# A decoder layer on one core: evacuation and background steps issued ahead of the weight split in each chunk

## The chip, the cores and the metric

The kernel runs on one core of a Trainium2 chip. The metric is the device time of one execution in microseconds (us), as the median of several runs. Before the change it is 2984.26 us (three runs, 2979.92 to 2984.27).

A core has a matrix engine (TensorE, PE in the profile, with its weight loads as PEld), a vector engine (VectorE, DVE), a scalar engine (ScalarE, ACT), GpSimd (POOL) and SyncE (SP), from whose queue nearly all DMAs of this kernel are issued. Each engine takes its instructions in the order in which the program wrote them, and waits on semaphores for what others owe it.

## The reference

One layer of a decoder, for 256 prompt tokens and 8 x 8 sample tokens, 320 token columns in all, with a model width of 2048:

```python
def swiglu(x, w_in, w_out):
    gate, up = jnp.split(x @ w_in, 2, axis=-1)
    return (jax.nn.silu(gate) * up) @ w_out

def token_mixer(h, w_in, ...):
    qk_pre, mv, mo, mif, aq, ak, av, gm, ga = split_cols(h @ w_in)
    # branch A: causal conv and SiLU of qk_pre, then a chunkwise mLSTM
    # branch B: dilated causal attention, of the prompt and over the cache
    merged = jax.nn.sigmoid(gm) * (hm @ w_pm) + jax.nn.sigmoid(ga) * (ha @ w_pa)
    return merged @ w_out, ...

x = x + 0.5 * swiglu(rmsnorm(x, ln_ffa), w_ffa_in, w_ffa_out)
x = x + token_mixer(rmsnorm(x, ln_mix), ...)
x = x + 0.5 * swiglu(rmsnorm(x, ln_ffb), w_ffb_in, w_ffb_out)
y = rmsnorm(x, ln_f)
```

Beside y, the new keys and values, the mLSTM state and the last convolution rows are returned.

## The kernel before

**Foreground.** Every product with a weight matrix is cut into jobs (`add_job`): a job gives 256 output columns for all 320 tokens, in one PSUM tile `fg` (two of them take turns). A job runs over its weights in chunks of up to four 128-row tiles, 512 KB of float32. `load_upto` fetches a chunk into one of four `raw` tiles. `split_upto` splits it into two parts that the matrix engine can take at full rate: ACT casts `raw` to `hi` (L223), DVE subtracts to get `lo` (L224); there are three `hi` and three `lo` tiles. For each tile pair PE then runs three matmuls (hi by x-high, hi by x-low, lo by x-high), so a full chunk has 24. The token side is split likewise: `xh`, `xl` for w_in, `hh`, `hl` in the feed-forward blocks, and `bh`, `bl` (`split_act`, L1345 and L1346) for the products with w_pm and w_pa.

**Order inside a chunk.** Nothing reorders the program; `run_job` (L270) writes it by hand. For chunk number ci it writes: the DMAs that were put off (`run_later`), the split of chunk ci+2, the background steps, then, in a job's first chunk (n == 0), the job's `setup` and the evacuation of the job before (`flush_evac`), then the load of chunk ci+6, then the matmuls of chunk ci. The load of ci+6 goes into the `raw` tile that the split of ci+2 read, so SP waits for that `lo`. The `hi` tile of chunk ci+2 is the one that chunk ci-1 read, so ACT waits for PE there.

**Background.** Everything else is written as Python generators that advance by one stage at each step: list `every` in each chunk, `even` and `odd` in alternate chunks, `slow` in 8 of 15. They carry the attention over the cache (`sample_attention`: `kd` transposes at L626, `qbd` at L674, scores `ss` from L701 on), the mLSTM (`mlstm`: state `C` at L1167, `ks`, `qm`, `kw`) and the later stages of evacuations. `flush_evac` runs an evacuation up to its first `yield` and puts the rest into `every`. Two kinds matter here:

- `sigmoid_evac` (20 jobs: mo, gm, ga): DVE multiplies by `rstd` (L395, tile `sg`), ACT takes an exponential (L998), POOL adds one (L999); then after a yield DVE takes the reciprocal of one half (L1002), after another yield that of the other.
- `mv_evac` (four jobs) and its like: DVE multiplies by `rstd` (L395, tile `mv`), two yields, then PE transposes the result (`tok_major`, L332).

**Openings.** The products with w_pm and w_pa begin with a `setup` (`pm_open`, `pa_open`) that splits the mLSTM's result `hr` and the attention's result `ar`. The first of four pieces of each is split earlier by a generator (`presplit`); the other three are split by `take` (L1356) in the setup itself.

**Sequence.** Feed-forward block a (chunks 0 to 271), the mixer's projection w_in with nearly all background work (272 to 448), w_pm (449 to 464), w_pa (465 to 480), w_out, feed-forward block b. In the first five chunks `first_chunk` stands in the place of the split and prepares the input.

Of the kernel before, what the change touches and what calls it, by code (L numbers as in the profile page):

```python
# [128 lines left out]
def decoder_kernel(tc, I, O, K):  # L129
# [13 lines left out]
    def mm(out, a, b, start=True, stop=True, **kw):  # L143
        T.matmul(out, a, b, start=start, stop=stop, **kw)  # L144
# [16 lines left out]
    def run_later(force=False):  # L161
        rest = []
        for e in later_q:
            e[0] -= 1
            if e[0] <= 0 or force:
                e[1]()
            else:
                rest.append(e)
        later_q[:] = rest
# [4 lines left out]
    def step(lst):  # L174
        for g in list(lst):
            try:
                next(g)
            except StopIteration:
                lst.remove(g)

    def spawn(g, lst=None, first=False):
        lst = every if lst is None else lst
        lst.insert(0 if first else len(lst), g)

    RAWB, HLB, KRB = 4, 3, 3
# [4 lines left out]
    def load_upto(n):  # L190
        while st["loaded"] < min(n, len(chunks)):
            i = st["loaded"]
            src, nk, kind = chunks[i]
            t = wp.tile([128, 4, 256], F32, tag="raw", bufs=RAWB, name="raw")
            if kind == "mif":
                v = t.rearrange("p a b -> p (a b)")[:, :128].rearrange("p (k c) -> p k c", k=16)
                dma(v, src)
            else:
                dma(t[:, :nk], src)
            raw[i] = t  # L200
            st["loaded"] += 1

    def split_upto(n):
        while st["split"] < min(n, len(chunks)):
            i = st["split"]
            load_upto(i + 1)
            src, nk, kind = chunks[i]
            hi = wp.tile([128, 4, 256], F32R, tag="hi", bufs=HLB, name="hi")
            lo = wp.tile([128, 4, 256], F32R, tag="lo", bufs=HLB, name="lo")
            t = raw.pop(i)  # L210
            if kind == "mif":
                G.memset(hi.bitcast(F32), 0.0)
                G.memset(lo.bitcast(F32), 0.0)
                r = t.rearrange("p a b -> p (a b)")[:, :128].rearrange("p (k c) -> p k c", k=16)
                h = hi.rearrange("p a b -> p (a b)").rearrange("p (k c) -> p k c", k=16)
                l = lo.rearrange("p a b -> p (a b)").rearrange("p (k c) -> p k c", k=16)
                for o, s in ((0, 0), (32, 4)):
                    S.copy(h[:, :, o:o + 4], r[:, :, s:s + 4])
                    V.tensor_tensor(l[:, :, o:o + 4], r[:, :, s:s + 4], h[:, :, o:o + 4].bitcast(F32),
                                    op=OP.subtract)  # L220
                wh[i], wl[i] = h, l
            else:
                S.copy(hi[:, :nk], t[:, :nk])  # L223
                V.tensor_tensor(lo[:, :nk], t[:, :nk], hi[:, :nk].bitcast(F32), op=OP.subtract)  # L224
                wh[i], wl[i] = hi, lo
            st["split"] += 1
# [22 lines left out]
    def fg_tile():  # L249
        return pp.tile([128, 2, 512], F32, tag="fg", bufs=2, name="fg")  # L250
# [7 lines left out]
    def flush_evac():  # L258
        if pending[0] is not None:
            evac, ps = pending[0]  # L260
            pending[0] = None
            g = evac(ps)
            if g is not None:
                try:
                    next(g)
                    every.append(g)
                except StopIteration:
                    pass

    def run_job(job):  # L270
        cs, nkt, mov, evac, kind, setup = job
        ps = fg_tile()
        for n, (ci, k0, nk) in enumerate(cs):
            run_later()
            if ci < 5:
                first_chunk(ci, 0)
            else:
                split_upto(ci + HLB)
            if tick[0] % 2 == 0:
                step(even)  # L280
            else:
                step(odd)
            tick[0] += 1
            pace[0] += 8
            if pace[0] >= 15:
                pace[0] -= 15
                step(slow)
            step(every)
            if n == 0 and setup is not None:
                setup()  # L290
            if ci == 7 or (n == 0 and ci != 4):
                flush_evac()
            load_upto(ci + HLB + RAWB)
            h, l = wh.pop(ci), wl.pop(ci)
            for m in range(1 if kind == "mif" else 2):
                if m and ci < 3:
                    first_chunk(ci, 1)
                for k in range(nk):
                    xh, xl = mov(k0 + k)
                    if kind == "mif":  # L300
                        a, b, out = h[:, k], l[:, k], ps[0:64, 0, 0:NT]
                    else:
                        a, b, out = h[:, k, m * 128:(m + 1) * 128], l[:, k, m * 128:(m + 1) * 128], ps[:, m, 0:NT]
                    first, last = k0 + k == 0, k0 + k == nkt - 1
                    mm(out, a, xh, start=first, stop=False)
                    mm(out, a, xl, start=False, stop=False)
                    mm(out, b, xh, start=False, stop=last)
        pending[0] = (evac, ps)
# [1024 lines left out]
    for j in range(8):  # L1333
        add_job(w_in, 0, 16, C_GA + j * 256, mov_x, lambda ps, j=j: sigmoid_evac(ps, gate_d[8 + j]),
                setup=(lambda: spawn(presplit("hr"))) if j == 7 else None)
# [15 lines left out]
    def presplit(key):  # L1351
        while key not in M:
            yield
        PRE[key] = split_act(M[key][0], t_tile)
# [5 lines left out]
    def pm_setup(j):  # L1360
        if j == 7:
            spawn(presplit("ar"))
        if j == 0:
            pm_open()
        load_pair(j, gate_d[j], t_tile(F32, "sg"))

    def pa_setup(j):
        if j == 0:
            pa_open()
        load_pair(j, gate_d[8 + j], ft_tile("sg"))  # L1370
# [56 lines left out]
    for j in range(8):  # L1427
        add_job(I["w_pm"][0], 0, 8, j * 256, mov_b, lambda ps, j=j: pm_evac(ps, j),
                setup=lambda j=j: pm_setup(j))
    for j in range(8):  # L1430
        add_job(I["w_pa"][0], 0, 8, j * 256, mov_b, lambda ps, j=j: pa_evac(ps, j),
                setup=lambda j=j: pa_setup(j))
# [57 lines left out]
    def warm(n):  # L1490
        ps = bg_tile()
        for _ in range(n):
            mm(ps[:, 0:128], ones, ones)
# [7 lines left out]
    def prep_pair(j, fg=False):  # L1501
        xv, c0, g0 = xl[j // 2], (j % 2) * 256, G_FFA + 2 * j
        X[j] = fp.tile([128, 2, NT], F32, tag="x", bufs=8, name="x")
        XH[j], XL[j] = t_tile(F32R, "xh"), t_tile(F32R, "xl")
        ft = fg_tile() if fg else None
        ps = [ft[:, 0], ft[:, 1]] if fg else [bg_tile(), bg_tile()]
        for m in range(2):
            for t in range(2):
                tr(ps[m][:, t * 128:(t + 1) * 128], xv[:, t, c0 + m * 128:c0 + (m + 1) * 128])
            tr(ps[m][:, SEQ:SEQ + 128], xv[:, 2, c0 + m * 128:c0 + (m + 1) * 128])  # L1510
        V.tensor_copy(X[j][:, 1], ps[1][:, 0:NT])
        for m in range(2):
            S.activation(XH[j][:, m], ps[m][:, 0:NT], AF.Copy, scale=gv[:, g0 + m:g0 + m + 1])
            if m == 0:
                S.copy(X[j][:, 0], ps[0][:, 0:NT])
        for m in range(2):
            V.scalar_tensor_tensor(XL[j][:, m], ps[m][:, 0:NT], gv[:, g0 + m:g0 + m + 1],
                                   XH[j][:, m].bitcast(F32), op0=OP.mult, op1=OP.subtract)

    def first_chunk(n, m):  # L1520
        if n == 0 and m == 0:
            prep_pair(0)
            prep_pair(1)
            split_upto(1)
            prep_pair(2, True)
            warm(8)
        elif n < 3:
            prep_pair(2 * n + 2 + m)
            if m == 1:
                split_upto(n + 2)  # L1530
        elif m == 0:
            split_upto(n + 2)
# [86 lines left out]
    for job in jobs:  # L1619
        run_job(job)  # L1620
# [56 lines left out]
```

## Time and profile before

| what | value |
|---|---|
| three runs: median, lowest, highest | 2984.26, 2979.92, 2984.27 us |
| the profiled execution's own time | 2982.11 us |
| its span (first to last instruction) | 2980.3 us |
| PE busy | 2933.2 us, 98% |
| DVE busy | 1625.1 us, 55% |
| ACT busy | 1095.6 us, 37% |
| mean granted PE clock | 0.994 |

A line of a view by groups reads: source line, engine, operation, output tile <- input tiles, shapes, count | busy us, mean ns of one | idle us of the engine just before them, and what ended it. A line of the timeline reads: start us, length us, engine, line, operation, tiles, shapes, count, and in brackets the idle time before it and who ended it. A line of the waits reads: engine, tile and line that waited <- who ended it: total us, times, longest us. A line of the windows reads: from:to in us, length, busy us of an engine (instructions), granted PE clock, DMA share, GB/s. In all of them L144 is the helper for matmuls, L332 that for transposes and L141 that for DMAs, so the tiles tell which is meant.

### The profile page before, as it was taken

The page shows a single profiled execution, that of the slowest core. Times are in us where ns is not written, and L with a number is a line of the kernel's source. Part 1 is how long each engine was busy: PE and PEld are TensorE (multiplying, and loading weights), DVE is VectorE, ACT ScalarE, POOL GpSimd, SP SyncE. Part 2 cuts the span into 40 slices and gives each one's busy share as a digit, 9 for nine tenths or more (in the row PEclk, how much of TensorE's full clock was granted, in tenths as well). Part 3 has the DMA queues.
Part 4 walks back from the last instruction along what each step waited for, and adds up shares of the span by engine and source line. Part 5 has one row for each costly group of instructions (what it writes and reads, how often), then busy time and mean ns, then how long its engine had stood idle before and what let it go on. Part 6 is the DMA issues. An engine that isn't in the chain of part 4 may idle for free.

```text
span 2980.3 us, 49081 instructions
## 1 busy us (share of the span) xinstructions
PE 2933.2 (98%) x20430; PEld 2849.2 (96%) x20430; DVE 1625.1 (55%) x1875; ACT 1095.6 (37%) x1383; POOL 225.8 (8%) x253
## 2 busy tenths in 40 slices
PE   9999999999999999999899999999999999999998
PEld 8999999999999999888788898999999999999998
DVE  5444444444446556878788875655444444444444
ACT  5332333333334333444443433334333332333334
POOL 1000000000000000132222210000000000000000
PEclk9999999999999999999999999999999999999999
DMA  6454444444446788899999986554444444444443
GB/s 193 151 159 155 149 149 150 151 149 147 154 145 188 216 232 253 237 287 299 276 278 312 302 270 212 181 171 153 149 150 150 152 150 149 149 148 153 152 140 116
DMA packets 507467, 557.09 MB, mean 187 GB/s; under 512 B 30124, under 2 KB 452060, under 8 KB 507220
## 3 DMA queue, kind: packets, MB, share of 16 engines
q1 hardware_dynamic: 507068, 553.87, 60.4%
q8 instruction: 160, 2.62, 0.4%
q14 instruction: 63, 0.52, 0.0%
q10 hardware_dynamic: 176, 0.07, 0.0%
HBM read 521.58 MB, written 32.28 MB: 186 GB/s over the span
## 4 chain that ended last, share of the span: by engine, by line
PE 93%; DMA 3%; DVE 2%; SPq 1%; issue 1%; ACT 0%; POOL 0%; DVEq 0%; ACTq 0%; POOLq 0%
PE fg L144 87%; PE bg L144 5%; PE bg L332 1%; DMA raw<-in_w_in_dram 1%; DMA vt<-in_cache_v_dram 1%; SPq L141 1%; DVE lo L224 0%; DMA kraw<-in_cache_k_dram 0%; DMA k<-qk_d 0%; ACT hi L223 0%; DMA xl<-in_x_prompt_dram 0%; DMA vq<-vm_d 0%; DVE kd L626 0%; DMA raw<-in_w_pm_dram 0%; DVE sg L1002 0%
## 5 line engine op out<-in xcount | busy, mean ns | idle before, releaser
L224 DVE TENSOR_TENSOR lo<-raw,hi 128x1024 fp32r<-128x1024 f32 (+1 forms) x784 | 967.7, 1235 | 1217.4 <-ACT hi L223 1203.7
L144 PE MATMUL fg<-xh,hi 128*128 128x320 f32 x4240 | 1321.8, 312 | 0.3 <-ACT hi L223 0.3
L144 PE MATMUL fg<-xh,lo 128*128 128x320 f32 x4240 | 1311.9, 309 | 2.7 <-DVE lo L224 2.7
L144 PE MATMUL fg<-xl,hi 128*128 128x320 f32 x4240 | 1311.1, 309 | 0.0
L223 ACT CAST hi<-raw 128x1024 fp32r<-128x1024 f32 (+1 forms) x784 | 806.2, 1029 | 1363.5 <-PE fg L144 1024.0
L144 PEld LDWEIGHTS fg<-xh,lo 128*128 128x128 f32 x4240 | 796.2, 188 | 4.3 <-DVE lo L224 4.2
L144 PEld LDWEIGHTS fg<-xh,hi 128*128 128x128 f32 x4240 | 796.8, 188 | 3.2 <-issue 1.3
L144 PEld LDWEIGHTS fg<-xl,hi 128*128 128x128 f32 x4240 | 796.7, 188 | 1.0 <-issue 0.2
L144 PE MATMUL fg<-hh,hi 128*128 128x320 f32 x1408 | 436.9, 310 | 0.0
L144 PE MATMUL fg<-hh,lo 128*128 128x320 f32 x1408 | 435.1, 309 | 0.0
L144 PE MATMUL fg<-hl,hi 128*128 128x320 f32 x1408 | 435.0, 309 | 0.0
L144 PEld LDWEIGHTS fg<-hl,hi 128*128 128x128 f32 x1408 | 264.3, 188 | 0.7 <-issue 0.7
L144 PEld LDWEIGHTS fg<-hh,hi 128*128 128x128 f32 x1408 | 264.3, 188 | 0.7 <-issue 0.7
L144 PEld LDWEIGHTS fg<-hh,lo 128*128 128x128 f32 x1408 | 264.3, 188 | 0.0
L439 POOL TENSOR_TENSOR gt<-gt,rstd 128x640 f32<-128x640 f32 x44 | 69.2, 1573 | 1880.7 <-ACT gt L438 1880.7
L144 PE MATMUL fg<-bh,hi 128*128 128x320 f32 x512 | 160.2, 313 | 1.5 <-ACT bh L1345 1.5
L144 PE MATMUL fg<-bl,hi 128*128 128x320 f32 x512 | 159.8, 312 | 1.9 <-DVE bl L1346 1.9
L144 PE MATMUL fg<-bh,lo 128*128 128x320 f32 x512 | 159.6, 312 | 0.0
L626 DVE STREAM_TRANSPOSE kd<-kraw 128x512 f32<-128x512 f32 x160 | 102.1, 682 | 8.0 <-DMA kraw<-in_cache_k_dram 7.9
L144 PEld LDWEIGHTS fg<-bh,hi 128*128 128x128 f32 x512 | 97.3, 190 | 3.7 <-ACT bh L1345 2.0
L144 PEld LDWEIGHTS fg<-bl,hi 128*128 128x128 f32 x512 | 97.4, 190 | 2.4 <-DVE bl L1346 2.4
L144 PEld LDWEIGHTS fg<-bh,lo 128*128 128x128 f32 x512 | 97.3, 190 | 0.0
(301 smaller groups left out, 1473.1 us busy)
## 6 DMA issues: line engine op xcount, KB each, us to landing
raw<-in_w_ffa_in_dram SPq DMA_DIRECT2D x176, 512.0 KB
raw<-in_w_in_dram SPq DMA_DIRECT2D x176, 512.0 KB
raw<-in_w_ffb_in_dram SPq DMA_DIRECT2D x176, 512.0 KB
raw<-in_w_ffa_out_dram SPq DMA_DIRECT2D x80, 512.0 KB
raw<-in_w_ffb_out_dram SPq DMA_DIRECT2D x80, 512.0 KB
kraw<-in_cache_k_dram SPq DMA_DIRECT2D x96, 256.0 KB
vt<-in_cache_v_dram SPq DMA_DIRECT2D x128, 192.0 KB
kraw<-in_cache_k_dram SPq DMA_DIRECT2D x32, 512.0 KB
```

The costliest lines, as they stand in the source:

```text
L141: nc.sync.dma_start(out, in_)
L144: T.matmul(out, a, b, start=start, stop=stop, **kw)
L223: S.copy(hi[:, :nk], t[:, :nk])
L224: V.tensor_tensor(lo[:, :nk], t[:, :nk], hi[:, :nk].bitcast(F32), op=OP.subtract)
L332: T.transpose(out, in_, ident[:k, :k])
L439: G.tensor_tensor(gt, gt, bcast(rstd, 2), op=OP.mult)
L626: V.transpose(kd[:, 2 * pr + g], t[:, g])
```

## The change

In each chunk the setup, the evacuation and the background steps are written first, and the split comes after them. The evacuation now stands ahead of the steps, so that its generator, put into `every`, makes its second stage in the same chunk. The load, the matmuls and all numbers of buffers stay.

```diff
@@ run_job
             run_later()
-            if ci < 5:
-                first_chunk(ci, 0)
-            else:
-                split_upto(ci + HLB)
+            if n == 0 and setup is not None:
+                setup()
+            if ci == 7 or (n == 0 and ci != 4):
+                flush_evac()
             if tick[0] % 2 == 0:
                 step(even)
             else:
                 step(odd)
...
             step(every)
-            if n == 0 and setup is not None:
-                setup()
-            if ci == 7 or (n == 0 and ci != 4):
-                flush_evac()
+            if ci < 5:
+                first_chunk(ci, 0)
+            else:
+                split_upto(ci + HLB)
             load_upto(ci + HLB + RAWB)
```

How that moves instructions is seen at three places. The first is ACT's queue at the opening of w_pm, where `bh<-hr` are the four casts of the mLSTM's result and `hi<-raw` the weight casts (a minus marks rows of before, a plus rows of the changed program):

```order
 L1345 CAST bh<-hr 128x640
-L223 CAST hi<-raw 128x1024 x3
+L223 CAST hi<-raw 128x1024 x4
 L1345 CAST bh<-hr 128x640 x3
 L998 ACTIVATE sg<-sg 128x640
-L223 CAST hi<-raw 128x1024 x2
 L762 COPY osb<-bg 128x512
 L223 CAST hi<-raw 128x1024
```

Before, the three weight casts between are those of chunks 449, 450 and 451; now the four are those of 447 to 450. So the last three `bh` no longer stand behind the cast of chunk 451, which waits for PE to end chunk 448. At w_pa the same holds one stage later.

The second place is DVE's queue in the evacuation of the fifth ga job, at its next job's first chunk; before:

```order
L395 TENSOR_TENSOR sg<-fg,rstd 128x640
L224 TENSOR_TENSOR lo<-raw,hi 128x1024
L626 STREAM_TRANSPOSE kd<-kraw 128x512 x2
L1002 RECIPROCAL sg<-sg 128x320
L224 TENSOR_TENSOR lo<-raw,hi 128x1024
L1216 TENSOR_TENSOR hh<-hh,re 128x640
L1218 SCALAR_TENSOR_TENSOR hh<-hh,gv,sgm 128x320 x2
L1002 RECIPROCAL sg<-sg 128x320
L224 TENSOR_TENSOR lo<-raw,hi 128x1024 x2
```

and in the changed program:

```order
L395 TENSOR_TENSOR sg<-fg,rstd 128x640
L1216 TENSOR_TENSOR hh<-hh,re 128x640
L1218 SCALAR_TENSOR_TENSOR hh<-hh,gv,sgm 128x320 x2
L1002 RECIPROCAL sg<-sg 128x320
L224 TENSOR_TENSOR lo<-raw,hi 128x1024
L1002 RECIPROCAL sg<-sg 128x320
L224 TENSOR_TENSOR lo<-raw,hi 128x1024 x2
```

The first reciprocal, which needs the exponential of ACT and the addition of POOL, has moved from behind the chunk's `lo` to ahead of it, with no weight split between it and the multiplication by `rstd`.

The third is DVE's queue around the evacuation of the second mv job; before:

```order
L798 COPY cw<-bg 4x128
L224 TENSOR_TENSOR lo<-raw,hi 128x1024
L626 STREAM_TRANSPOSE kd<-kraw 128x512 x4
L395 TENSOR_TENSOR mv<-fg,rstd 128x640
L224 TENSOR_TENSOR lo<-raw,hi 128x1024
```

and in the changed program:

```order
L805 TENSOR_TENSOR cw<-cw 4x32x4
L224 TENSOR_TENSOR lo<-raw,hi 128x1024
L395 TENSOR_TENSOR mv<-fg,rstd 128x640
L626 STREAM_TRANSPOSE kd<-kraw 128x512 x2
L224 TENSOR_TENSOR lo<-raw,hi 128x1024
```

The evacuation is now the first thing of its chunk, and the key transposes and the weight split come behind it. The transposes of `mv` on PE come one chunk sooner after it than before.

## The prediction

> **What bounds the kernel now.** The page's first part comes first: PE is busy for all but 47 us of the span.
>
> ```profile
> PE 2933.2 (98%) x20430; PEld 2849.2 (96%) x20430; DVE 1625.1 (55%) x1875; ACT 1095.6 (37%) x1383; POOL 225.8 (8%) x253
> ```
>
> So a change of order can win only what PE loses, and the next question is where. The view by windows gives it by stage (busy us of PE, PEld, DVE, ACT and POOL, with their instructions, then the granted clock, the DMA share and GB/s):
>
> ```profile
> 45.00:961.00 916.00, 916.00 (x6231) 911.86 (x6230) 419.46 (x396) 312.01 (x332) 38.88 (x30) 1.00 0.49 153
> ...
> 1160.00:1300.00 140.00, 131.35 (x981) 118.30 (x980) 106.01 (x184) 54.12 (x94) 18.29 (x30) 0.98 0.87 247
> 1300.00:1500.00 200.00, 188.07 (x1396) 165.54 (x1395) 163.36 (x252) 87.68 (x148) 57.04 (x80) 0.97 0.94 282
> 1500.00:1700.00 200.00, 194.66 (x1462) 174.79 (x1461) 163.44 (x212) 87.75 (x141) 51.10 (x64) 0.99 1.00 305
> ...
> 1864.20:2906.00 1041.80, 1041.58 (x7103) 1041.15 (x7101) 484.46 (x448) 362.27 (x385) 34.71 (x22) 1.00 0.49 154
> ```
>
> Feed-forward block a (45 to 961) and all from 1864 to 2906 leave PE no idle time at full clock: there the change is worth nothing as long as it makes PE wait for nothing. The idle time lies in the mixer, from 1160 to 1700: 8.65 + 11.93 + 5.34 = 25.9 us, with the clock a little down and, at the end, the DMA engines always busy. The view of waits, of PE from 961 to 1870, names whom PE waits for:
>
> ```profile
> PE bg L332 <- DVE mv L395: 6.4, 3, 2.9
> PE bg L144 <- POOL qbd L674: 6.0, 1, 6.0
> PE bg L144 <- ACT kw L1121: 4.0, 1, 4.0
> PE bg L144 <- POOL ks L1065: 2.2, 2, 2.0
> PE bg L332 <- ACT cs L990: 2.0, 1, 2.0
> PE fg L144 <- DVE bl L1346: 1.9, 2, 1.0
> PE bg L144 <- ACT osb L821: 1.8, 1, 1.8
> PE bg L144 <- POOL qm L1054: 1.6, 1, 1.6
> PE fg L144 <- ACT bh L1345: 1.5, 2, 0.7
> ```
>
> Nearly all are waits of background work, not of weights: the split is early, evacuations and steps are late. That is what the change trades.
>
> **Term 1, the two openings.** The windows, for PE alone, of the first chunk of w_pm, of the two chunks ahead of w_pa, and of w_pa's first:
>
> ```profile
> 1791.80:1799.08 7.28, 5.59 (x27) 0.77 0.86 284
> 1849.92:1856.96 7.04, 7.04 (x50) 1.00 0.88 303
> 1856.96:1864.24 7.28, 5.59 (x26) 0.77 0.58 189
> ```
>
> Two ordinary chunks take 7.04 us (48 matmuls; the two above that overlap the edges), so one takes 3.52; an opening chunk takes 7.28. Each opening loses 3.76 us. The timeline of PE, ACT and DVE at w_pa shows why:
>
> ```profile
> 1853.49 1.05 ACT L223 CAST hi<-raw 128x1024 fp32r<-128x1024 f32 x1 [2.47 <-PE fg L144]
> 1857.01 1.05 ACT L223 CAST hi<-raw 128x1024 fp32r<-128x1024 f32 x1 [1.84 <-PE fg L144]
> 1857.96 1.97 ACT L1345 CAST bh<-ar 128x640 fp32r<-128x640 f32 x3
> 1854.57 1.23 DVE L224 TENSOR_TENSOR lo<-raw,hi 128x1024 fp32r<-128x1024 f32 x1 [1.56 <-ACT hi L223]
> 1859.23 2.29 DVE L1346 TENSOR_TENSOR bl<-ar,bh 128x640 fp32r<-128x640 f32 x3
> 1858.74 0.42 PE L144 MATMUL fg<-bh,hi 128*128 128x320 f32 x1 [0.74 <-ACT bh L1345]
> 1860.11 0.64 PE L144 MATMUL fg<-bl,hi 128*128 128x320 f32 x1 [0.95 <-DVE bl L1346]
> 1860.54 0.47 PE L144 MATMUL fg<-bh,lo 128*128 128x320 f32 x1
> 1860.81 0.47 PE L144 MATMUL fg<-bh,hi 128*128 128x320 f32 x1
> ```
>
> The three `bh` stand on ACT behind the cast of a later weight chunk, which waits for PE to finish the chunk before. With the split behind the setup they follow the cast that begins at 1853.49: 1854.5 to about 1856.5, and the `bl` follow the `lo` that ends at 1855.8, to 1858.1, the first of them by 1856.6. PE needs the second piece at 1856.96 plus six matmuls, 1857.8. If the last piece still has to wait for PE to leave chunk 464, it is ready by 1858.6, and it is not read before chunk 466, at 1860.5. At w_pm it is the same with the cast of chunk 450 in place of the one at 1853.49:
>
> ```profile
> 1788.37 1.05 ACT L223 CAST hi<-raw 128x1024 fp32r<-128x1024 f32 x1 [2.47 <-PE fg L144]
> 1789.46 1.23 DVE L224 TENSOR_TENSOR lo<-raw,hi 128x1024 fp32r<-128x1024 f32 x1
> ```
>
> `bh` by 1791.4, the first `bl` by 1791.5, needed at 1792.7. Both openings lose their waits: -3.76 x 2 = **-7.5 us**. The idle time itself is 1.7 us each; the other 2.1 us are matmuls spaced 0.27 us (1860.54 to 1860.81) at a granted clock of 0.77 in that window, where 7.04 / 48 = 0.147 is the rule.
>
> [...]
>
> **Term 2, the start.** In the waits of 30 to 60 us stands one of the row sums of squares, which now come ahead of two splits on DVE:
>
> ```profile
> PE bg L144 <- DVE ss L377: 0.5, 1, 0.5
> ```
>
> It goes: **-0.5 us**, between 0 and that. What moves back for it are only the splits of the next chunks, of which no wait of PE shows one.
>
> **Term 3, background waits in the mixer.** An example of the largest row, from DVE's timeline:
>
> ```profile
> 1262.94 2.48 DVE L626 STREAM_TRANSPOSE kd<-kraw 128x512 f32<-128x512 f32 x4
> 1265.35 0.78 DVE L395 TENSOR_TENSOR mv<-fg,rstd 128x640 f32<-128x640 f32 x1
> ```
>
> The evacuation stood behind a `lo` and four transposes; now it is first in its chunk. But PE's transposes of it come one chunk sooner, so I count half: 3.2 of 6.4. The `ks`, `qm`, `cs` and `osb` rows (7.6 us) are ACT and POOL steps that stood behind a cast, or behind a late DVE; again half, 3.8. The `qbd` and `kw` rows (10 us) I leave: `qbd` needs a chain of small DMAs and `kw` is one wait of 4.0 us, in the stretch of key loads. With the slower matmuls behind each wait (2.2 times the wait in term 1, less where waits are short; I take 1.4) the term is -7.0 x 1.4 = **-10 us**. Bounds: 0 if each wait only moves, -34 if all seven rows (24.0 us) go at that factor.
>
> **Term 4, weights that come late.** The price is that the split's `lo` stands behind the chunk's steps. The sigmoid jobs are the hard case, for DVE now waits inside the chunk. One of them before:
>
> ```profile
> 1709.85 0.78 DVE L395 TENSOR_TENSOR sg<-fg,rstd 128x640 f32<-128x640 f32 x1
> 1710.66 0.74 ACT L998 ACTIVATE sg<-sg 128x640 f32<-128x640 f32 x1 [3.01 <-DVE sg L395]
> 1711.55 1.81 POOL L999 TENSOR_SCALAR sg<-sg 128x640 f32<-128x640 f32 x1 [2.90 <-issue]
> 1713.51 2.14 DVE L1002 RECIPROCAL sg<-sg 128x320 f32<-128x320 f32 x1
> ```
>
> From the multiplication's start to POOL's end is 3.5 us (1709.85 to 1713.36); a reciprocal of 2.14 and a `lo` of 1.23 make 6.9 us after PE ends the job before. Other steps of DVE fit into its 2.7 us of waiting. The weights are needed two chunks after that: 7.04 us at the least, and on average
>
> ```profile
> L224 DVE TENSOR_TENSOR lo<-raw,hi 128x1024 fp32r<-128x1024 f32 x145 | 178.5, 1234 | 118.9 <-ACT hi L223 116.3 <-PE bg L144 2.3
> ```
>
> 145 chunks in the 700 us from 1160 to 1860, 4.83 us a chunk, 9.7 for two. So it fits if DVE is less than 2.8 us behind when the job ends. The same row says what DVE gains: 118.9 us idle in front of `lo`, waiting for a cast that waited for PE; steps can now fill that. Bounds: 0, and 20 jobs x 1 us late x 2.2 = +44. I take the end that is nearer to the row: a fifth of the jobs late by 1 to 2 us and a few dense mLSTM chunks beside, **+8 us**.
>
> Waits that the change adds to queues: the load of chunk ci+6 waits on SP for the `lo` of ci+2, and whatever SP issues next stands behind it. From 1160 to 1860 that is already SP's largest wait, and the casts already wait for loads at times:
>
> ```profile
> SPq L141 <- DVE lo L224: 133.3, 69, 6.9
> ACT hi L223 <- DMA raw<-in_w_in_dram: 30.5, 10, 6.7
> ```
>
> Key loads keep their place in time, since they wait for both the `kd` transposes and that `lo` either way. Weight loads leave later by a chunk's steps, 2 to 3 us. I count it at nothing, because four loads are out at a time, 4 x 4.83 = 19 us; where the engines are at 1.00 that cover is thin (rival B).
>
> Outside the mixer an evacuation puts such an operation or two ahead of a split with 7.04 us to go:
>
> ```profile
> L460 DVE SCALAR_TENSOR_TENSOR x<-fg,x 128x640 f32<-128x640 f32 x48 | 39.2, 818 | 0.0
> ```
>
> With a `lo` of 1.23 us and a cast of 1.05 behind it that fits: nothing.
>
> **Sum.** -7.5 - 0.5 - 10 + 8 = -10.0 against the profiled execution's 2982.11: 2972.1. That execution stands 2.15 us below the median of 2984.26, inside the spread of the three runs (4.3); I predict 2973.
>
> **Rivals.**
> - *A, slower: the sigmoid chain sets the pace.* Place: the first chunk of the 20 jobs behind a sigmoid job. If DVE is more than 2.8 us behind there, `lo` is late, PE waits a microsecond or so and runs slow behind it, 2.2 us a job. It decides from about half the jobs on: 10 x 2.2 = +22 and the background waits that only moved (term 3 at 0): 2982.1 - 8 + 22 = 2996. For it: DVE is over 80% busy between 1300 and 1700, by far the tightest engine beside PE. Against it: the 118.9 us idle in front of `lo`.
> - *B, no change: what goes comes back.* Later `lo` means later loads; the ten waits for weights, 30.5 us, lie where the DMA engines are at 0.87 to 1.00. Each longer by 2.5 us, and half of that reaching PE, is +12, against term 3's -10 the sum is 2982.1 - 8 - 10 + 8 + 12 = 2984. The openings staying as they are, if their tiles come free too late, gives 2972.1 + 7.5 = 2980, the same class.
> - *C, much faster: DVE's idle time fills.* Term 3 at 24.0 x 1.4 = -34 with term 4 at 0: 2982.1 - 8 - 34 = 2940; half way to it, 2957, is what I would expect of this case.
>
> **How the numbers follow.** Forecast (2964 to 2978) 0.40, A 0.25, B 0.20, C 0.15. About 0.2%, 6 us, is what a measurement of this kernel can tell from no change: faster is below 2978 (forecast and C, 0.55), the same is B (0.20), slower is A (0.25). The range 2953 to 3000 leaves out the deeper half of C and the part of A in which most of the 20 jobs are late.
>
> **What would show it.** Step by step: the first chunk of w_pm and of w_pa takes 3.5 us at clock 1.00, and the `bh` and `bl` rows are gone from PE's waits; `mv` is less than half its 6.4 us there; DVE's idle time in front of `lo` in the mixer is well below 118.9. A new row of PE `fg` waiting for DVE `lo`, above some 10 us, would show A; more than 30.5 us of ACT waiting for `raw`, with SP's wait for `lo` above 133.3, would show B. Any idle time of PE from 1864 to 2906 would prove the cover outside the mixer wrong.

## The result, and the profile after

The changed kernel takes 3009.88 us (median of four runs, 3007.59 to 3015.18), against 2984.27 before: a ratio of 1.0096, 95% interval 1.0084 to 1.0109. The median is 26 us higher, where 2973 was forecast. One of the four executions before took 7401.76 us and is left out of the ratio. The profiled execution took 3008.74 us, 26.6 more than the one before.

The engines' part of the page shows the same numbers of instructions in a longer span:

```profile
PE 2942.8 (98%) x20430; PEld 2857.5 (95%) x20430; DVE 1634.5 (54%) x1875; ACT 1093.0 (36%) x1383; POOL 217.4 (7%) x253
```

The windows (columns as before: busy us of PE, PEld, DVE, ACT, POOL, the granted clock, DMA share, GB/s) are the same stretches as before, with the first chunk of w_pm and of w_pa at their new times:

```profile
45.00:961.00 916.00, 916.00 (x6231) 911.86 (x6230) 424.40 (x398) 310.80 (x331) 38.92 (x30) 1.00 0.50 153
1160.00:1300.00 140.00, 130.11 (x947) 116.86 (x946) 101.56 (x179) 51.68 (x92) 15.00 (x31) 0.96 0.86 246
1300.00:1500.00 200.00, 180.30 (x1286) 160.42 (x1288) 158.35 (x242) 82.84 (x141) 49.83 (x77) 0.94 0.92 272
1500.00:1700.00 200.00, 187.32 (x1381) 166.01 (x1377) 154.73 (x197) 81.63 (x132) 47.01 (x59) 0.97 0.92 277
1828.51:1832.27 3.76, 3.76 (x31) 3.67 (x27) 1.01 (x2) 2.16 (x3) 1.81 (x1) 1.00 0.65 238
1887.11:1890.63 3.52, 3.52 (x26) 3.52 (x25) 2.91 (x4) 1.05 (x1) 0.00 (x0) 1.00 0.69 240
```

Feed-forward block a is untouched. The two openings are mended: 3.76 and 3.52 us in place of 7.28 each, at a granted clock of 1.00. What was lost lies in the mixer: PE idles 9.9 + 19.7 + 12.7 = 42.3 us between 1160 and 1700, where it idled 25.9, and the clock there is lower by 0.02 to 0.03. By stages, w_in's first chunk starts 1.0 us earlier, the time from there to w_pm's first chunk is 37.7 us longer, w_pm and w_pa together take 10.3 us less and the rest 0.2 more. The view of waits, of PE from 961 to 1890, names the new one:

```profile
PE fg L144 <- DVE lo L224: 29.5, 14, 4.7
PE bg L144 <- POOL qbd L674: 5.3, 1, 5.3
PE bg L144 <- DMA k<-qk_d: 4.2, 1, 4.2
PE fg L144 <- ACT hi L223: 2.2, 3, 1.6
PE bg L332 <- issue: 1.9, 1, 1.9
PE bg L332 <- DVE mv L395: 1.1, 1, 1.1
```

The background waits that the change was expected to shorten are shorter (mv 6.4 to 1.1; kw, cs, osb and qm gone from the list), and weights are now what PE waits for most. In the same view, from 1160 to 1887, ACT, SP and DVE:

```profile
ACT hi L223 <- DMA raw<-in_w_in_dram: 55.0, 17, 8.4
...
SPq L141 <- DVE lo L224: 176.4, 60, 9.7
...
DVE lo L224 <- ACT hi L223: 49.0, 32, 4.6
DVE ss L701 <- PE bg L144: 42.8, 11, 12.2
DVE kd L626 <- DMA kraw<-in_cache_k_dram: 20.3, 12, 9.3
DVE sg L1002 <- POOL sg L999: 16.5, 11, 2.7
DVE z L1073 <- DMA re<-rows_d: 11.3, 3, 7.8
```

DVE's idle time moved from in front of `lo` (116.3 before, to 1860) to in front of background steps (before, `ss` was 18.8, `kd` 7.9 and `z` 2.8); SP waits longer for `lo` (133.3 before) and ACT nearly twice as long for `raw` (30.5 before).

Two late weights, read from DVE's timeline. In the first, DVE goes from an evacuation (`pre`) straight through key transposes, a reciprocal and half a convolution (`y`), and reaches the `lo` of chunk 335 at 1233.39; PE, further down, had stood still for 2.99 us:

```profile
1225.19 0.68 DVE L942 TENSOR_TENSOR pre<-fg,rstd 128x512 f32<-128x512 f32 x1
1225.90 0.29 DVE L944 TENSOR_TENSOR pre<-fg,rstd 128x128 f32<-128x128 f32 x1
1226.11 1.29 DVE L626 STREAM_TRANSPOSE kd<-kraw 128x512 f32<-128x512 f32 x2
1227.33 2.11 DVE L972 RECIPROCAL pre<-pre 128x320 f32<-128x320 f32 x1
1229.36 4.10 DVE L964 SCALAR_TENSOR_TENSOR y<-pre,gv,y 128x256 f32<-128x256 f32 x6
1233.39 1.21 DVE L224 TENSOR_TENSOR lo<-raw,hi 128x1024 fp32r<-128x1024 f32 x1
...
1234.65 0.41 PE L144 MATMUL fg<-xh,lo 128*128 128x320 f32 x1 [2.99 <-DVE lo L224]
```

In the second DVE itself waits, 9.33 us for key loads, with `lo` behind their transposes, and PE stands still for 3.30 us:

```profile
1272.54 0.15 DVE L1086 TENSOR_TENSOR eb<-mixc,aeT 128x8 f32<-128x8 f32 x1
1282.02 0.71 DVE L626 STREAM_TRANSPOSE kd<-kraw 128x512 f32<-128x512 f32 x1 [9.33 <-DMA kraw<-in_cache_k_dram]
1282.96 0.71 DVE L626 STREAM_TRANSPOSE kd<-kraw 128x512 f32<-128x512 f32 x1 [0.23 <-DMA kraw<-in_cache_k_dram]
1283.60 1.18 DVE L224 TENSOR_TENSOR lo<-raw,hi 128x1024 fp32r<-128x1024 f32 x1
...
1284.83 0.42 PE L144 MATMUL fg<-xh,lo 128*128 128x320 f32 x1 [3.30 <-DVE lo L224]
```

From such rows the first theory was made: weights are late because DVE has too much to do ahead of `lo` (theory L). The rival was that the harm is done on SP, where the next weight load waits for that late `lo` (theory D).

### The profile page after: what moved, and what is told of

Read it like the earlier page. It is cut to its first block, busy times and chain, and to the rows that moved or that the text cites. A ratio compares the mean times of both kernels' runs of the same rounds, so it can differ in the third digit from the quotient of the medians.

```text
span 3007.0 us, 48913 instructions
## 1 busy us (share of the span) xinstructions
PE 2942.8 (98%) x20430; PEld 2857.5 (95%) x20430; DVE 1634.5 (54%) x1875; ACT 1093.0 (36%) x1383; POOL 217.4 (7%) x253
## 4 chain that ended last, share of the span: by engine, by line
PE 86%; DMA 6%; DVE 4%; issue 1%; SPq 1%; ACT 1%; POOL 0%; DVEq 0%; ACTq 0%; POOLq 0%
PE fg L144 81%; PE bg L144 4%; DMA raw<-in_w_in_dram 1%; DMA vt<-in_cache_v_dram 1%; DVE lo L224 1%; DMA kraw<-in_cache_k_dram 1%; SPq L141 1%; PE bg L332 1%; DVE pre L972 1%; DVE kd L626 0%; DVE y L964 0%; ACT hi L223 0%; DVE sg L1002 0%; DMA re<-rows_d 0%; DMA C<-in_state_C_dram 0%
## 5 line engine op out<-in xcount | busy, mean ns | idle before, releaser
L144 PE MATMUL fg<-xh,lo 128*128 128x320 f32 x4240 | 1319.6, 311 | 31.8 <-DVE lo L224 31.4
L626 DVE STREAM_TRANSPOSE kd<-kraw 128x512 f32<-128x512 f32 x160 | 102.8, 683 | 20.4 <-DMA kraw<-in_cache_k_dram 20.3
```

Of the source, the lines that this page charges most:

```text
L626: V.transpose(kd[:, 2 * pr + g], t[:, g])
```

## The experiments

All ratios are to the kernel before, on the same chip; differences in us are between medians. The rows come from several chips, on which the median of the kernel before lay between 2980.46 and 2984.27 us, so a difference between rows of less than some 4 us says nothing without the ratios. In the table X is the split, P the steps, E the evacuation, in the order in which a chunk issues them; in all but the first row the setup comes first.

| order or change | us | ratio (95% interval) |
|---|---|---|
| before: X, P, setup, E | 2984.27 | |
| the change: setup, E, P, X | 3009.88 | 1.0096 (1.0084 to 1.0109) |
| X P E (o_xpe) | 2973.71 | 0.9977 (0.9967 to 0.9987) |
| P E X (o_pex) | 3016.30 | 1.0124 (1.0107 to 1.0141) |
| P X E (o_pxe) | 3009.96 | 1.0108 (1.0087 to 1.0129) |
| E X P (o_exp) | 2985.57 | 1.0015 (1.0002 to 1.0029) |
| X E P (o_xep) | 2994.63 | 1.0040 (1.0028 to 1.0053) |
| X E P, second stage a chunk later (xep_nomerge) | 2978.51 | 0.9983 (0.9974 to 0.9992) |
| E P X, convolution a chunk later (c_qk) | 3011.18 | 1.0109 (1.0092 to 1.0126) |
| cast, E, P, subtraction (hi_first) | 3009.69 | 1.0084 (1.0060 to 1.0107) |
| list every, X, other steps, E (ev_first) | 2986.61 | 1.0016 (1.0004 to 1.0028) |
| other steps, X, list every, E (bg_first) | 3000.87 | 1.0060 (1.0045 to 1.0075) |
| X P E, three raw tiles (xpe_raw3) | 2998.51 | 1.0057 (1.0040 to 1.0073) |
| X P E, loads held back (late_load) | 3000.89 | 1.0059 (1.0041 to 1.0076) |
| its control (copy_only) | 2974.50 | 0.9973 (0.9963 to 0.9983) |
| E P X, loads one chunk later, behind its DMAs (after_ln) | 2984.57 | 1.0012 (1.0001 to 1.0022) |
| X P E, loads behind the next chunk's put-off DMAs (xpe_ln) | 2989.03 | 1.0026 (1.0017 to 1.0036) |
| late_load, loads as in xpe_ln (late_load_ln) | 2989.04 | 1.0021 (1.0008 to 1.0033) |
| E P X, keys and values from ACT's queue (after_actq) | 3060.69 | 1.0261 (1.0244 to 1.0278) |
| X P E, the same (xpe_actq) | 3058.71 | 1.0253 (1.0238 to 1.0268) |

### Which of the moves costs

The first four put the three moves apart. **The setup alone** is moved here, against before:

```diff
             run_later()
+            if n == 0 and setup is not None:
+                setup()
             if ci < 5:
                 first_chunk(ci, 0)
...
-            if n == 0 and setup is not None:
-                setup()
             if ci == 7 or (n == 0 and ci != 4):
```

> The order of before (split, steps, evacuation), with only the setup ahead of the split. Both theories of the result say the same here: the first chunks of w_pm and w_pa take 3.5 us each in place of 7.28, PE waits for lo stay at about 2.7 us, and the time is 2984.3 - 7.5 = 2976.8 (2973 to 2980). If the openings were only shifted, it would be 2984.

2973.71, as expected: this part of the change is sound, and with its interval wholly below 1 (0.9977, some 7 us below before).

**The evacuation behind the steps again, or behind the split**, all else as changed:

```diff
-            if ci == 7 or (n == 0 and ci != 4):
-                flush_evac()
             if tick[0] % 2 == 0:
...
             step(every)
+            if ci == 7 or (n == 0 and ci != 4):
+                flush_evac()
             if ci < 5:
                 first_chunk(ci, 0)
```

> Setup, steps, evacuation, split: the split is as late as in the changed kernel, but an evacuation's second stage comes one chunk later, as before. Theory L (lo is late because of the DVE work that stands ahead of it, above all the two stages of one evacuation that now share a chunk: 11.9 of the 31.4 us of waits for lo lie in four convolution chunks, 7.9 in five sigmoid chunks): waits for lo fall to about 12 us and the time by 20 x 1.4 = 28 us to about 2982 (2976 to 2989). Rival D (weights are late because their loads leave later, since SP's wait for lo grew from 133 to 176 us and ACT's for raw from 30.5 to 55.0): the split is as late, so waits for lo stay above 22 us, ACT's for raw above 45 us, and the time is above 2998.

and in the second with the same two lines behind `split_upto(ci + HLB)`:

> Setup, steps, split, evacuation: the evacuation stays behind the split, the steps are ahead of it. Theory L: no merged stages and less work ahead of lo; waits for lo about 8 us, the background waits of PE as before (the mv row near 6 us), time about 2982 (2975 to 2988). Rival D: ACT's wait for raw above 45 us and a time above 2995.

Both miss: 3016 and 3010. Theory L in its first form, that the merged stages make the weights late, is wrong; the steps ahead of the split cost the same 36 to 43 us over X P E wherever the evacuation stands. The convolution moved a chunk later (in `qk_evac`) says the same:

```diff
         yield
+        yield
         y = t_tile(F32, "y")
```

> The changed kernel with one more yield in the qk evacuation, between its multiplications by rstd and its convolution, so that the convolution comes one chunk later again; all else as changed. Theory L: the four waits for lo in mo0.2, mo1.2, mo2.2, mo3.2 (2.99 + 1.75 + 4.73 + 2.41 = 11.9 us) go, and the time falls by 11.9 x 1.4 = 17 us to 2993 (2986 to 2998). Rival D: less than 5 us, 3005 or more.

3011.18. The four waits that it aimed at are gone from their chunks, and others stand one chunk on; PE waits 27.9 us for `lo` in place of 31.4 over the whole run. D had the times of all three right, and in P E X the waits for `lo` (above 22 us expected, 32.1 measured), but not ACT's for `raw`: they were to stay above 45 us in P E X and P X E, and were 41.8 and 42.5.

With the split ahead of the steps, the evacuation's place was next. Against the change, first behind the evacuation:

```diff
                 flush_evac()
+            if ci < 5:
+                first_chunk(ci, 0)
+            else:
+                split_upto(ci + HLB)
             if tick[0] % 2 == 0:
...
-            if ci < 5:
-                first_chunk(ci, 0)
-            else:
-                split_upto(ci + HLB)
             load_upto(ci + HLB + RAWB)
```

> Setup, evacuation, split, steps: only the evacuation's first stage is ahead of the split, the steps are behind it. Theory L2 (formed after the four runs before: it isn't the merged stages but the steps as a whole that make lo late, since a chunk's background work on DVE often takes longer than the 4.7 us between the cast and the need of the weights): waits of PE for lo below 6 us, the mv row at about 1 us, as in the changed kernel, and a time 3 to 5 us below that of the order split, steps, evacuation, so 2965 to 2973 beside 2973.7. If the evacuation ahead of the split is what costs, waits for lo above 20 us and 3000 or more.

and with the same four lines ahead of it:

> Setup, split, evacuation, steps: the split is as early as before, but an evacuation shares its chunk with its second stage, as in the changed kernel. Theory L2: waits for lo below 6 us, time 2968 to 2978. If the merged stages by themselves made the background slower (first multiplication, exponential, addition and reciprocal in a row), the time would be above 2985.

Both miss, 12 and 21 us above X P E. To see whether the merged stage does it, the generator joins the list `every` only behind the chunk's steps:

```diff
-                    every.append(g)
+                    (fresh if defer else every).append(g)
...
             step(every)
+            every.extend(fresh)
+            fresh.clear()
```

> Setup, split, evacuation, steps as in the run of 2994.6 us, but the evacuation's generator joins the list every behind that chunk's steps, so that its second stage comes a chunk later again. Theory M (the merged second stage takes a chunk of distance away, and PE reaches rstd's sums and mv before they are ready): the time returns to 2970 to 2980, the ss L381 and mv waits of PE fall from 11.5 us to below 6. Rival (the evacuation itself, ahead of the steps, delays the attention's and the mLSTM's steps): 2988 or more.

2978.51, so 16 of the 21 us were the merge: the yields of an evacuation are distances between one engine's result and another's use of it, and the merge takes one away. No single row of PE's waits carries it: the rows named fell from 11.5 to 6.0 us, at the edge of what was expected (mv from 6.4 to 0.9, ss stayed at 5.1), while qbd grew from 3.9 to 8.1. With the split last the cost doesn't show: the merged order (3009.88) is no slower than the unmerged one (3016.30), though there the evacuation's place differs too.

**Which steps.** Against X P E, one group of steps is put ahead of the split. First the list `every`:

```diff
+            step(every)
             if ci < 5:
                 first_chunk(ci, 0)
...
                 step(slow)
-            step(every)
```

> Only the list every (the later stages of evacuations) is stepped ahead of the split; attention and mLSTM steps stay behind it, and the evacuation last. Theory L2 in numbers of DVE time: a chunk with a convolution half (4 us) or a reciprocal (2.1 us) ahead of its lo has 4.7 us to spare, so hardly any lo is late: waits for lo below 10 us, time 2975 to 2985. If the convolution and sigmoid stages are what makes lo late (as in the four runs with the split last), waits for lo stay above 20 us and the time is above 2995.

and then the lists `even`, `odd` and `slow`, with `every` behind the split:

> The complement: attention and mLSTM steps (even, odd, slow) ahead of the split, the list every behind it, and the evacuation last. They hold DVE's waits for other engines and DMAs (for kraw, re, cn, the scores on PE), which lo then inherits. If those waits are the larger part: above 2990 with waits for lo above 15 us. If it takes both groups in one chunk to make lo late: 2975 to 2987, waits for lo below 12 us.

The evacuations' later stages cost 13 us (PE's waits for `lo` 11.9 us over the whole run, a little over the bound), attention and mLSTM 27 (22.7 us), and both together (P X E) 36. The group that waits for transfers and other engines is the dearer one.

**ACT or DVE.** The cast goes first again, the subtraction stays last:

```diff
+            if ci >= 5:
+                split_upto(ci + HLB, True)
             if ci == 7 or (n == 0 and ci != 4):
...
-            else:
-                split_upto(ci + HLB)
+            while held:
+                held.pop(0)()
```

> The changed kernel with the split cut in two: ACT's cast to hi is issued first in the chunk, as before, and DVE's subtraction to lo last, as changed. Theory L2 (DVE's order is what counts): waits for lo above 20 us and a time of 3000 to 3015. Rival H (the casts came late, behind ACT operations that wait for DVE, and lo behind them): lo waits below 10 us and a time below 2990.

3009.69: the order on ACT is not what costs. It is the subtraction's place, and with it the time at which a raw tile comes free.

### What the late subtraction does

**Loads one chunk later, split early**: X P E with three raw tiles.

```diff
-    RAWB, HLB, KRB = 4, 3, 3
+    RAWB, HLB, KRB = 3, 3, 3
```

> The order split, steps, evacuation with the setup ahead (2973.7 us), but with three raw tiles in place of four, and the load of chunk ci+5 in place of ci+6: each load is issued one chunk later, the split stays early. Theory L2 (loads that leave a few us later cost little): below 2982, ACT's wait for raw up by less than 25 us. Rival D (the changed kernel is slow because its loads leave later): ACT's wait for raw above 55 us and a time above 2995.

2998.51, so D could not be dropped. But there each load moves by a whole chunk. The run that follows holds each load until DVE is through with the chunk's steps, as the changed kernel does, and leaves `hi` and `lo` early: DVE reads eight numbers of the raw tile behind the steps and the evacuation.

```diff
                 flush_evac()
+            while seen:
+                V.tensor_copy(scr, seen.pop(0)[0:1, 0, 0:8])
             load_upto(ci + HLB + RAWB)
```

> The order split, steps, evacuation with the setup ahead (2973.7 us), with one addition: DVE reads eight numbers of the raw tile behind the chunk's steps and evacuation, so that the load into that tile leaves as late as in the changed kernel, while hi and lo stay early. DVE has some 780 such copies more, of about 0.1 us. Theory L2 (what costs is lo behind the steps on DVE): 2974 to 2985, waits of PE for lo below 6 us. Rival D (what costs is that the weight loads leave later): 2995 or more, ACT's wait for raw above 45 us. Between 2985 and 2995 both have a share, to be read as the excess over 2973.7 against the 36 us of the changed kernel.

In the control the copy reads `ones[0:1, 0:8]` in place of the raw tile:

> Control for the run with the late loads (3000.9 us): the same small copies on DVE at the same places, but of a constant, so that no load waits for them. Theory D (later loads cost the 27 us there): 2972 to 2980, within 6 us of the 2973.7 without copies. Rival C (the copies themselves, some 23 us of DVE time between 1160 and 1887 us, are the cost): 2992 or more.

3000.89 with the hold, 2974.50 with the same copies of a constant: **holding the loads costs 26 us by itself**, with PE waiting little for weights. Its waits (ACT and SP from 1160 to 1887, PE from 961 to 1890):

```profile
ACT hi L224 <- DMA raw<-in_w_in_dram: 103.1, 30, 10.9
...
SPq L141 <- DVE scr L296: 244.4, 76, 9.7
...
PE bg L144 <- POOL qbd L679: 12.1, 2, 10.3
PE fg L144 <- DVE lo L225: 6.8, 6, 3.9
PE bg L337 <- DVE scr L296: 5.7, 3, 2.9
PE bg L144 <- ACT osb L826: 4.6, 1, 4.6
```

PE's largest is not a weight. `qbd` is the attention's query tile, which waits for small transfers (in the changed kernel POOL stood idle ahead of it for 8.8 us, for `q<-qs_d`); they stand on SP, where loads now wait 244.4 us. (That is a longer hold than the changed kernel's 176.4, and the control has 117.4 and 50.4 for `lo` and the copies, so the 26 us need not be the changed kernel's share.) (The `scr` row is the mv row under another name, since the copy comes behind it.)

So the next runs let the small transfers pass. Each load is written into SP's program one chunk later, behind the DMAs that were put off to that chunk, and waits for the same `lo`. In the changed kernel, shown here, it then stands behind the DMAs that the chunk's steps issue at once as well (`k`, the rows, the store of the queries); in the two runs after it the load stands ahead of the split and the steps, so behind the put-off DMAs alone:

```diff
+            load_upto(ci + HLB + RAWB - 1)
             if ci < 5:
                 first_chunk(ci, 0)
             else:
                 split_upto(ci + HLB)
-            load_upto(ci + HLB + RAWB)
```

> The changed kernel with each weight load issued one chunk later in SP's program, ahead of that chunk's split: it waits for the same lo, but the small DMAs put off to that chunk (keys, values, stores) now stand ahead of it. Theory Q (the harm of a late lo on SP is to the transfers queued behind the load: keys, rows, qk): at least 10 us less than the changed kernel, 2999 or below. Theory W (the harm is to the weights, which come late themselves): 3005 to 3025.

> The same move of the loads in the order split, steps, evacuation with the setup ahead (2973.7 us). Theory Q: the same or a little faster, 2966 to 2975. Theory W: slower, 2978 to 2995.

> The run with the late loads (3000.9 us) with the same move of the loads past the next chunk's put-off DMAs. Theory Q: most of the 27 us goes, 2988 or below. Theory W: 2997 to 3015.

The changed kernel comes back from 3009.88 to 2984.57, and the one with the held loads from 3000.89 to 2989.04, a little above the 2988 that was expected. In X P E a like move costs 15 us, which is theory W's answer: the weights lose a chunk of lead, and ACT's wait for `raw` goes from 26.5 to 84.0 us. So both happen, and in the changed kernel the transfers behind the load weigh more: with the loads out of their way, the split last (2984.57) is no slower than the split first (2989.03), though the loads don't stand at quite the same place. The pair that differs in the hold alone is the clearest: with the loads moved, holding them (2989.04, SP still waiting 212.0 us for the copies) costs nothing over not holding them (2989.03), where it cost 26 us before. In the changed kernel with this move DVE no longer waits noticeably for `kraw` (0.7 us in place of 20.3), nor PE noticeably for `qbd` and `k`, while 21.0 us of waits for `lo` remain:

```profile
PE fg L144 <- DVE lo L224: 21.0, 13, 4.6
PE fg L144 <- ACT hi L223: 5.7, 4, 2.5
PE bg L332 <- issue: 1.8, 1, 1.8
PE bg L332 <- DVE mv L395: 1.0, 1, 1.0
PE bg L144 <- DVE ss L381: 0.8, 1, 0.8
PE bg L144 <- POOL qbd L674: 0.8, 1, 0.8
```

The last pair was to tell which transfers matter, by issuing key and value loads from ACT's queue:

```diff
             t = mxt([128, 2, 512], "kr", KRB, "kraw")
...
-                dma(t, raw_ap(ck, off + (1536 + 2 * pr) * 1024, [[4096, 128], [1024, 2], [1, 512]]))
+                S.dma_start(t, raw_ap(ck, off + (1536 + 2 * pr) * 1024, [[4096, 128], [1024, 2], [1, 512]]))
```

> The changed kernel with the loads of keys and values (load_k, load_v) issued from ACT's queue in place of SP's, so that they no longer stand behind a weight load that waits for lo; the weight loads keep their place. Theory Q: DVE's wait for kraw (20.3 us) and part of the waits behind it go, 2985 to 2999; ACT may lose some of that where it waits to issue. Theory W: no better than 3005.

> The same move of the key and value loads in the order split, steps, evacuation with the setup ahead (2973.7 us). Theory Q: there the loads are hardly held, so little is to be won: 2966 to 2978. If ACT's own issuing and waiting costs more than that: above 2980, and the run with the changed order must be read with that difference taken off.

Inconclusive: both are near 3060, because ACT, which now issues them in its own order, stands still for them. In X P E its cast waits behind value loads for

```profile
ACT hi L223 <- DMA vt<-in_cache_v_dram: 91.6, 25, 7.4
```

That the two orders differ by 2 us there says nothing, since another limit rules both.

**What stays open.** Which of the transfers behind a held load does the harm: keys, the rows, `k` or the query tile. And what the late `lo` would cost if no load waited for it: a fifth raw tile would show it, and no run here has one.

## Why the prediction was wrong, step by step

- **Terms 1 and 2, right.** The openings gave 7.28 - 3.76 + 7.28 - 3.52 = 7.3 us against the 7.5 forecast, and X P E, which holds only term 1 (PE's wait for `ss` of 0.5 us is still in it), is faster than before (0.9977). At the start that wait is gone in the changed kernel, and the first chunks gained 0.7 against 0.5.
- **Term 3, right in its rows, not shown as time.** Of the seven rows (24.0 us) mv, qbd and ks remain with 1.1 + 5.3 + 0.7 = 7.1; two new ones, `k` 4.2 and a wait for issue 1.9, take part of it back. So 10.8 us of waits went, against 7.0. But the evacuation ahead of the steps didn't bring that by itself: with the weights early, the background waits of PE rise from 22.4 us in X P E to 30.0 in E X P and 29.9 in X E P, and the time by 12 and 21 us. The half taken off because PE's use comes one chunk sooner was too little; the second stage in the same chunk alone costs 16 us there.
- **Outside the mixer, right.** Block a has no idle time and the time from w_out on grew by 0.2 us.
- **Term 4 is the step that failed**, in two places. The first is the sentence on queues: "Weight loads leave later by a chunk's steps, 2 to 3 us. I count it at nothing, because four loads are out at a time". It priced the weights alone. The load that waits holds everything behind it on SP, and DVE waits for some of that with the next `lo` behind it, so the lateness can feed itself: `lo` late, load held, keys and rows late, DVE waiting, `lo` late. One such place is seen: with the small transfers let pass, DVE's 9.33 us for keys at 1282 becomes 0.45, and PE's 3.30 us for the `lo` behind it 0.36. Holding the loads alone cost 26 us, and letting the small transfers pass gave back 25 of the changed kernel's 36 us over X P E. The section even had the row for it, SP's 133.3 us of waiting for `lo`, and said that whatever SP issues next stands behind the load, but it looked only at the key loads, where it found cover ("Key loads keep their place in time").
- The second is the estimate of +8 for late `lo`, from 20 sigmoid jobs. PE waited 29.5 us for `lo` in 14 places, and by the timeline a sigmoid's reciprocal stood last in line in seven of them (13.2 us), a convolution in four (11.9). The row of 118.9 us idle in front of `lo` was read as room to fill. It was the room of chunks that had little to do; a chunk with 8 us of steps gets no share of it.
- **Rival A** (2996) had the side, the new row and a part of the places. But its chain isn't needed for the loss: in P E X, where the first reciprocal comes a chunk later again, the time is 3016.30. **Rival B** had the right place: ACT's wait for `raw` rose to 55.0 and SP's for `lo` to 176.4, as it said. It was priced at +12, with half of the wait reaching PE at no slower clock, and with nothing behind the loads. That its 2984 is also the time of the changed kernel with that blocking taken out is chance: 21.0 us of waits for `lo` remain there, which B doesn't have.
- **The price of a wait** was mis-sized too. From w_in's first chunk to w_pm's first, before and after (for PE alone: busy us, granted clock, DMA share, GB/s):

```profile
961.14:1791.80 830.66, 804.46 (x5980) 0.99 0.90 269
960.11:1828.51 868.40, 822.29 (x6004) 0.97 0.88 258
```

  PE's idle time rose from 26.2 to 46.1 us, by 19.9, and the time by 37.7 us, 1.9 times as much. The other 17.8 us are PE's busy time, 822.29 us in place of 804.46 for the same matmuls, at a granted clock of 0.97 in place of 0.99. The 2.2 of term 1 was nearer to that than the 1.4 of term 3.
- On the clock term 1 rested on one kind of place, the openings, where waits of 0.74 and 0.95 us stand in a window at 0.77. The runs again show a wait below 2 us at such a clock, one of 1.75 us in a window at 0.76 (below); but one of 2.88 us in a window at 1.00 shows that the length alone doesn't decide.

## What to carry to other kernels

When an instruction is moved back in its queue, ask not only who reads its result, but which queue waits for the buffer that it frees, and list everything that stands behind that wait. On SP's queue here a waiting load delayed transfers that have nothing to do with it: holding the loads cost 26 us (3000.89 against 2974.50), and nothing once the put-off DMAs stood ahead of them (2989.04 against 2989.03). A total of idle time in front of a step, here 118.9 us, is no room for moved work: look at the busiest chunks; and a `yield` between stages is a distance that other engines need, so an earlier start that removes one can cost more than it brings (16 us in X E P).

## What the runs showed of the hardware

The same kind of wait of PE, for a `lo` in the middle of a chunk, did not always cost the same. Here are a wait of 1.75 us and one of 1.28 in the changed kernel, with the windows of their chunks (for PE alone), and one of 2.88 in P X E:

```profile
1320.16 0.49 PE L144 MATMUL fg<-xh,lo 128*128 128x320 f32 x1 [1.75 <-DVE lo L224]
1694.43 0.41 PE L144 MATMUL fg<-xh,lo 128*128 128x320 f32 x1 [1.28 <-DVE lo L224]
```

```profile
1317.96:1325.03 7.07, 5.32 (x27) 0.76 1.03 332
1692.69:1697.82 5.13, 3.85 (x27) 1.00 1.04 361
```

```profile
1425.60 0.42 PE L144 MATMUL fg<-xh,lo 128*128 128x320 f32 x1 [2.88 <-DVE lo L224]
...
1422.26:1429.06 6.80, 3.92 (x30) 1.00 1.02 303
```

A full chunk takes 3.52 us. The first took 7.07, which is 1.8 us more than chunk and wait, at a granted clock of 0.76; the second 0.3 more, at 1.00; the third 0.4 more, at 1.00. The wait of 2.99 us at 1234.65 in the changed kernel is like the first: its window, 1231.20 to 1239.51, is 8.31 us long, 1.8 us more than chunk and wait, at 0.79. So a wait of 2.88 us in P X E cost less beyond its own length than one of 1.75 us in the changed kernel, and of these four the two dear ones are those with a lower granted clock. What makes the clock differ between them is left open.
